# Two more key steps ahead of the value steps, key outputs in two pools, sample slots first in the gather

## The chip, the cores and the metric

One core of a Trainium2 chip runs the whole kernel. The metric is device time in microseconds (us) of one execution; lower is better. TensorE (PE) multiplies matrices, VectorE (DVE) and ScalarE (ACT) do elementwise work, GpSimd (POOL) does elementwise work and issues gathers, SyncE (SP) issues most loads.

## What is computed

One layer of a hybrid decoder, on 512 prompt tokens and 8 x 4 = 32 sample tokens, all in float32. The first part (recurrence, state space, gates) is not touched here. The second part is an expert mixer with 8 heads and 128 x 128 = 16384 single-neuron experts:

```python
# per head: the 16 best of 128 x 128 key pairs by summed score -> expert, gate = softmax
act = gelu(einsum('thkd,td->thk', u_tab[expert], x))
out = einsum('thk,thkd->td', gate * act, v_tab[expert])
y = rmsnorm(x_residual + out, final_norm_w)
```

## The kernel before

The mixer handles the tokens in two ways. Prompt tokens 128 to 511 (three tiles of 128, `d_tiles`) are done densely: for each of NE = 128 keys e, that is 128 experts each, a **key step** (`h_step(e)`) multiplies table u of that key with the 384 tokens and puts the gelu into a tile `gh[e]` of 128 x 384; a **value step** (`v_step(e)`) multiplies `gh[e]` with the routing weights (`wt`, read in blocks of eight keys from a scratch `Wt` in DRAM) and adds the product with table v of that key to three accumulators in PSUM. Tables are split in two float32r halves (`thi` by a ScalarE cast, `tlo` by a VectorE subtraction), so a key step is 8 x 3 matmuls of 384 columns and a value step 3 x 3 x 2 of 512. The first prompt tile (128 tokens, 128 slots each) and the samples (32 tokens laid out four times over the partitions, 32 slots) are `g_tiles` and are done by gather: `gathered` walks over 160 slots, and for each GpSimd fetches 128 rows of u and v (1 MB, three slots ahead); one step is VectorE's product with the token (L1353, `uv`) and ScalarE's gelu and gate (`w`), the next is VectorE's `acc` (L1360). At the end of a tile the four copies of the samples are folded by matmuls with `sid`, copied, and `finish` adds the residual row, normalizes and stores.

Nothing is scheduled by a planner: each engine runs its instructions in the order in which the program emits them. Background work is Python generators in the queues `bg` and `fill`; `tick(rate)` adds the rate to a debt, and for each whole unit one generator makes one step. A key step has four ticks (after k = 1, 3, 5, 7), a value step three. So the rates set how many gathered steps lie between the matmuls of a key.

The order of the mixer: `experts` runs AH = 34 key steps **ahead**, between the router's work (lists, top-k, `combine`), the building of `Wt` (`build_w`) and the samples' lists. Up to e = AH - AW = 22 they stand in the router's loop at rate 1, then ten in the building of `Wt`, then the last two. Their outputs need AH tiles `gh`: AH - 3 in a pool `gha`, the last three in `ghp`. Then the value steps run alone (`G_AHEAD` = 0.38 per tick) until 31 are done; the pool is closed, its room goes to the tables of the later key steps (`dpu2`), keys 34 and 35 are fetched, and the last weights and five residual rows (`finish_load`) are loaded in one go. From there a **loop** does key step v + 1 and value step v in turn with rate `G_RATE`, which is worked out so that the gather ends with the loop. `v_last` does the last value step, finishes the dense tiles and drains what is left of the gather.

Of the kernel before, what the change touches and what calls it, by code (L numbers as in the profile page):

```python
# [8 lines left out]
F32 = mybir.dt.float32  # L9
# [10 lines left out]
P = 128  # L20
D = 1024
# [69 lines left out]
def body(tc, a):  # L91
# [7 lines left out]
    def pool(st, name, bufs=1, right=False, space=None):  # L99
        kw = {} if space is None else {"space": space}  # L100
        return st.enter_context(tc.tile_pool(name=name, bufs=bufs, side="right" if right else "left", reuse_waits="tile", **kw))

    def load(dst, src):
        nc.sync.dma_start(dst, src)
# [23 lines left out]
    T_ = {}  # L128
# [1175 lines left out]
                            sm.rearrange("p (a b) -> p a b", a=na).unsqueeze(3).to_broadcast([P, na, nb, 16]), ALU.mult)  # L1304


    def finish_load(fp, t, rows, x2):
        o = fp.tile([P, D], F32, name="fin", tag=f"fin{t}")
        load(o[:rows], x2)
        return o  # L1310

# [17 lines left out]
    def gathered(gp, ps_of, tiles):  # L1329

        slots = [(i, k) for i, t in enumerate(tiles) for k in range(t[1][2])]
        uvs, accs = {}, {}

        def fetch(j):
            if j < len(slots):
                i, k = slots[j]
                ei = tiles[i][1][0]
                uvs[j] = gp.tile([P, 2 * D], F32, name="uv", tag="uv", bufs=GA)
                PO.indirect_dma_start(out=uvs[j], out_offset=None, in_=a["uv"],  # L1339
                                      in_offset=bass.IndirectOffsetOnAxis(ap=ei[:, k : k + 1], axis=0))  # L1340

        for x in range(GA - 1):
            fetch(x)
        yield
        for j, (i, k) in enumerate(slots):
            rows, (ei, gate, n), h2, end = tiles[i]
            if k == 0:
                accs[i] = gp.tile([P, D], F32, name="acc", tag="acc", bufs=1)
            acc = accs[i]
            w = gp.tile([P, 1], F32, name="w", tag="w", bufs=4)  # L1350
            fetch(j + GA - 1)
            uv = uvs.pop(j)
            V.scalar_tensor_tensor(out=uv[:, 0:D], in0=uv[:, 0:D], scalar=1.0, in1=h2, op0=ALU.mult, op1=ALU.mult, accum_out=w)  # L1353
            AC.activation(w, w, AF.Gelu)  # L1354
            AC.mul(w, w, gate[:, k : k + 1])  # L1355
            yield
            if k == 0:
                AC.mul(acc, uv[:, D:], w)
            else:
                V.scalar_tensor_tensor(acc, uv[:, D:], w, acc, ALU.mult, ALU.add)  # L1360
            yield
            if k == n - 1:
                o2 = acc.rearrange("p (a b) -> p a b", a=2)
                if rows < P:
                    for b in range(2):
                        ps = ps_of()
                        mm(ps[:rows, :512], T_["sid"], acc[:, 512 * b : 512 * b + 512], start=True, stop=True)
                        yield
                        AC.copy(acc[:rows, 512 * b : 512 * b + 512], ps[:rows, :512])
                    yield  # L1370
                    o2 = acc[:rows].rearrange("p (a b) -> p a b", a=2)
                yield from end(o2)


    NE = 128
    AH = 34
    GA = 4
    VB = 3
    W0E = PO
# [11 lines left out]

    G_AHEAD = 0.38
    G_END = -8
    G_RATE = (2 * 160 + 12 - 3 * (AH - 1) * G_AHEAD) / (7 * (NE - AH) - 3 * G_END)

    def build_w(bp, pw, io, sls, Wt, w0):

# [40 lines left out]
    def experts(h2s, x2s, h2pair, ph, g_tiles, d_tiles, outs, s, ghp, es, sq):  # L1438
        nd = len(d_tiles)
        nt = nd * P  # L1440
        c0 = ph.p0 + d_tiles[0] - ph.t0
        Wt = dram.tile([nt // TB, P, P * TB], F32, name="Wt")
        st_ = ExitStack()
        ga = pool(st_, "gha")
        dps = ExitStack()
        dp = pool(dps, "dpu")
        php = pool(es, "php", 2, space=PSUM)
# [2 lines left out]
        def ps_h():  # L1450
            return php.tile([P, 512], F32, name="hps", tag="h")
# [3 lines left out]
        def fetch(kind, e):  # L1455
            if e < NE and (kind, e) not in raws:
                t = (dp if kind == "u" else dv).tile([P, D], F32, name="traw", tag="traw" + kind, bufs=2 if kind == "u" else VB)
                load(t, a["uT"][e] if kind == "u" else a["uv"][e * P : (e + 1) * P, D : 2 * D])
                raws[kind, e] = t
# [14 lines left out]
        def prep_lo(kind, e):  # L1474
            if e < NE and (kind, e) in raws:
                x, y = sp_[kind, e]
                (PO if kind == "u" and e < sum(AQ) else V).tensor_tensor(y, raws.pop((kind, e)), x, ALU.subtract)  # L1477
                if kind == "v" or e + 2 not in (AH, AH + 1) or e >= AH:
                    fetch(kind, e + (2 if kind == "u" else VB))

        gh = {}

        def h_step(e, rate, lo_at=0):
            prep("u", e)
            if e + 1 != AH:
                fetch("u", e + 1)
                prep("u", e + 1, True)
            x, y = sp_.pop(("u", e))
            ps = ps_h()
            for k in range(KT):  # L1490
                ks = slice(k * P, k * P + P)
                cs = slice(c0, c0 + nt)
                mm(ps[:, :nt], x[:, ks], hi[:, k, cs], start=(k == 0), stop=False)  # L1493
                mm(ps[:, :nt], x[:, ks], lo[:, k, cs], start=False, stop=False)  # L1494
                mm(ps[:, :nt], y[:, ks], hi[:, k, cs], start=False, stop=(k == KT - 1))  # L1495
                if k % 2:
                    (bg if e < AH else fill).tick(rate)
                if k == lo_at and e + 1 != AH:
                    prep_lo("u", e + 1)
            gh[e] = ga.tile([P, nt], F32, name="gh", tag="gh", bufs=AH - 3) if e < AH - 3 else ghp.tile([P, nt], F32, name="gh", tag="gh", bufs=3)  # L1500
            AC.activation(gh[e], ps[:, :nt], AF.Gelu)

        gs = {}
# [64 lines left out]
        e = 0  # L1568
# [60 lines left out]
        rows_of = {t: NS if t is None else P for t in g_tiles + d_tiles}  # L1629
        fins = {}  # L1630
        fill.add(gathered(gp, ps_h, [(rows_of[t], res[t], h2s[t], end_of(t, rows_of[t])) for t in g_tiles]))

        def v_of(v, rate):
            if v % 8 == 0:
                fetch_w(v // 8 + 1)
            v_step(v, rate)

        for v in range(AH - 3):
            v_of(v, G_AHEAD)
        st_.close()  # L1640
        dp = pool(es, "dpu2")
        fetch("u", AH)
        fetch("u", AH + 1)
        v_of(AH - 3, G_AHEAD)
        prep("u", AH)
        v_of(AH - 2, G_AHEAD)
        fp = T_["fp"] = pool(es, "fp")
        T_["fwbc"] = fp.tile([P, D], F32, name="fwbc")
        load(T_["fwbc"], a["fw"].to_broadcast([P, D]))
        for t in g_tiles + d_tiles:  # L1650
            fins[t] = finish_load(fp, t, rows_of[t], x2s[t])
        h_step(AH, G_RATE)
        for v in range(AH - 1, NE - NL):
            if AH < v + 1 < NE:
                h_step(v + 1, G_RATE)
            v_of(v, G_RATE)
        for v in range(NE - NL + 1, NE):
            h_step(v, G_RATE)
        v_last(range(NE - NL, NE))
        es.close()  # L1660

    outs = {None: a["o_y_s"]}
    for t in range(0, SEQ, P):
        outs[t] = a["o_y_p"][t : t + P]
    ph = Phase(0, True, 0, SEQ, True)
    g_tiles, d_tiles = [0, None], [128, 256, 384]
    es, sq = ExitStack(), ExitStack()
    wq = Stream(None, None, [(WQ0 + i, None, 0, None, PO) for i in range(16)], 4, Q_RATE, 0)
    h2s, x2s, h2pair, ghp = network(ph, g_tiles, wq, es, sq)
# [94 lines left out]
```

## Time and profile before

| | us |
|---|---|
| time, median of 3 runs | 2227.87 (2227.82 to 2234.36) |
| time of the profiled execution | 2235.91 |
| its span, first to last instruction | 2234.2 |
| PE busy, of the span | 2112.2 (95%) |
| DVE busy | 1578.4 (71%) |
| ACT busy | 848.8 (38%) |
| mean granted clock of TensorE, as a share | 0.981 |

The profile gives each engine's instructions with start and length. Matmuls overlap and their ends are modelled, so a TensorE that is busy all the time is not necessarily at its peak; distances between starts are the safer measure. The ahead stage lies at about 885 to 1237 us, the value steps alone at 1237 to 1382, the loop at 1382 to 2208.

### The profile page before, as it was taken

The numbers are of one execution on the slowest core, as the hardware profiler recorded it, in microseconds if no ns is written. First come the engines' busy times: TensorE is split into PE (matmuls) and PEld (weight loads), VectorE is DVE, ScalarE is ACT, GpSimd is POOL, SyncE is SP. The second block draws the span as 40 slices with busy tenths as digits, with TensorE's granted clock in tenths as the row PEclk, the third lists the DMA queues.
The fourth block names the chain that finished last, engine by engine and source line by source line (L and its number), as shares of the span: only waits on it lengthen the run. The fifth ranks groups of instructions, "written<-read, shape, count | busy, mean of one in ns | idle before, by whom it ended". The sixth has DMA issues, their size and how long they took to land.

```text
span 2234.2 us, 34565 instructions
## 1 busy us (share of the span) xinstructions
PE 2112.2 (95%) x13085; PEld 1937.5 (87%) x13085; DVE 1578.4 (71%) x3056; ACT 848.8 (38%) x1583; POOL 815.8 (37%) x904
## 2 busy tenths in 40 slices
PE   7899998999999998999899999899999999999996
PEld 6889898898999998999799878788888888888885
DVE  6866566655445424799998778687778788777777
ACT  3323232333113324333477434343443433344343
POOL 3488762224443333664166111222222222222221
PEclk9999998999999999999999999999999999999998
DMA  4433344326644243232356979899889999888983
GB/s 147 121 111 119 123 126 137 113 100 186 200 134 129 88 151 121 81 109 68 111 227 260 332 276 331 308 335 334 326 309 333 334 331 333 309 330 312 331 300 148
DMA packets 199814, 478.90 MB, mean 214 GB/s; under 512 B 53440, under 2 KB 114752, under 8 KB 176096
## 3 DMA queue, kind: packets, MB, share of 16 engines
q1 hardware_dynamic: 169136, 278.50, 37.6%
q0 software_dynamic: 24752, 170.67, 20.3%
q10 hardware_dynamic: 5760, 27.53, 3.1%
q8 instruction: 103, 1.69, 0.3%
q14 instruction: 63, 0.52, 0.1%
HBM read 419.42 MB, written 54.46 MB: 212 GB/s over the span
## 4 chain that ended last, share of the span: by engine, by line
PE 53%; DVE 26%; issue 8%; ACT 7%; DMA 5%; POOL 1%; SPq 0%; DVEq 0%; POOLq 0%; ACTq 0%
PE gps L469 23%; PE eacc L1548 7%; DVE uv L1353 5%; DVE tlo L1477 5%; PE hps L1493 3%; PE hps L1495 3%; PE hps L1494 3%; DVE acc L1360 3%; ACT thi L1469 3%; PE pw L1428 3%; DMA traw<-in_uv 2%; DVE glo L483 2%; PE aps L605 1%; ACT w L1355 1%; PE py L790 1%
## 5 line engine op out<-in xcount | busy, mean ns | idle before, releaser
L469 PE MATMUL gps<-pr,wh 128*128 128x272 f32 (+1 forms) x3328 | 584.7, 298 | 5.8 <-DVE pr L483 3.2
L469 PEld LDWEIGHTS gps<-pr,wh 128*128 128x128 f32 x3328 | 481.7, 192 | 14.5 <-issue 4.4
L1477 DVE TENSOR_TENSOR tlo<-traw,thi 128x1024 fp32r<-128x1024 f32 x241 | 298.9, 1241 | 146.3 <-ACT thi L1469 146.3
L1339 POOL DMA_INDIRECT uv<-in_uv,ei x128 | 176.4, 1378 | 605.4 <-DVE acc L1360 578.1
L469 PE MATMUL gps<-pr,wl 128*128 128x272 f32 (+1 forms) x1664 | 354.4, 293 | 8.8 <-POOL wl L435 7.7
L1495 PE MATMUL hps<-pr,tlo 128*128 128x384 f32 x1024 | 348.5, 340 | 15.0 <-DVE tlo L1477 13.5
L1493 PE MATMUL hps<-pr,thi 128*128 128x384 f32 x1024 | 350.8, 343 | 8.6 <-ACT thi L1469 8.6
L435 POOL TENSOR_TENSOR wl<-wraw,wh 128x1024 fp32r<-128x1024 f32 x88 | 216.9, 2465 | 350.8 <-ACT wh L434 338.9
L1494 PE MATMUL hps<-pr,thi 128*128 128x384 f32 x1024 | 344.5, 336 | 0.0
L1469 ACT CAST thi<-traw 128x1024 fp32r<-128x1024 f32 x256 | 266.1, 1040 | 44.5 <-DMA traw<-in_uv 15.6
L469 PEld LDWEIGHTS gps<-pr,wl 128*128 128x128 f32 x1664 | 267.3, 192 | 9.9 <-POOL wl L435 8.2
L1548 PE MATMUL eacc<-thi,ghi 128*128 128x512 f32 x768 | 243.7, 398 | 10.6 <-ACT ghi L482 9.4
L1548 PE MATMUL eacc<-tlo,ghi 128*128 128x512 f32 x768 | 243.4, 398 | 4.1
L1548 PE MATMUL eacc<-thi,glo 128*128 128x512 f32 x768 | 238.5, 392 | 0.0
L1360 DVE SCALAR_TENSOR_TENSOR acc<-uv,w,acc 128x1024 f32<-128x1024 f32 x158 | 202.3, 1280 | 30.5 <-ACT w L1355 30.5
L1354 ACT ACTIVATE w<-w 128x1 f32<-128x1 f32 x160 | 32.5, 203 | 486.3 <-DVE uv L1353 486.3
L1495 PEld LDWEIGHTS hps<-pr,tlo 128*128 128x128 f32 x1024 | 192.9, 188 | 23.0 <-DVE tlo L1477 21.8
L1493 PEld LDWEIGHTS hps<-pr,thi 128*128 128x128 f32 x1024 | 193.4, 189 | 15.8 <-ACT thi L1469 10.7
L1494 PEld LDWEIGHTS hps<-pr,thi 128*128 128x128 f32 x1024 | 193.4, 189 | 3.6
L1353 DVE SCALAR_TENSOR_TENSOR uv<-uv,h 128x1024 f32<-128x1024 f32 x160 | 194.8, 1217 | 0.0
L1548 PEld LDWEIGHTS eacc<-tlo,ghi 128*128 128x128 f32 x768 | 141.9, 189 | 50.1 <-DVE tlo L1477 21.9
L1548 PEld LDWEIGHTS eacc<-thi,ghi 128*128 128x128 f32 x768 | 141.2, 189 | 46.6 <-ACT ghi L482 22.6
(405 smaller groups left out, 3021.5 us busy)
## 6 DMA issues: line engine op xcount, KB each, us to landing
traw<-in_uT SPq DMA_DIRECT2D x128, 512.0 KB
traw<-in_uv SPq DMA_DIRECT2D x128, 512.0 KB
wraw<-in_W SPq DMA_DIRECT2D x104, 512.0 KB
Wt<-wb ACTq DMA_DIRECT2D x24, 1024.0 KB
wt<-Wt SPq DMA_DIRECT2D x15, 1536.0 KB
st<-in_state_hgrn SPq DMA_DIRECT2D x8, 512.0 KB
Wd<-W SPq DMA_DIRECT2D x8, 512.0 KB
ATd<-AT SPq DMA_DIRECT2D x8, 512.0 KB
```

The costliest lines, as they stand in the source:

```text
L435: E.tensor_tensor(wl, r3, wh, ALU.subtract)
L469: mm(ps[:, b, :w], x[:, k], y[:, k, b * w : b * w + w], start=(k == 0 and x is wh and y is hi), stop=(k == KT - 1 and x is wl))
L1339: PO.indirect_dma_start(out=uvs[j], out_offset=None, in_=a["uv"], in_offset=bass.IndirectOffsetOnAxis(ap=ei[:, k : k + 1], axis=0))
L1353: V.scalar_tensor_tensor(out=uv[:, 0:D], in0=uv[:, 0:D], scalar=1.0, in1=h2, op0=ALU.mult, op1=ALU.mult, accum_out=w)
L1360: V.scalar_tensor_tensor(acc, uv[:, D:], w, acc, ALU.mult, ALU.add)
L1428: mm(pt[:, t], o2[:, t], o1[:, t], start=True, stop=True)
L1469: AC.copy(x, t)
L1477: (PO if kind == "u" and e < sum(AQ) else V).tensor_tensor(y, raws.pop((kind, e)), x, ALU.subtract)
L1493: mm(ps[:, :nt], x[:, ks], hi[:, k, cs], start=(k == 0), stop=False)
L1494: mm(ps[:, :nt], x[:, ks], lo[:, k, cs], start=False, stop=False)
L1495: mm(ps[:, :nt], y[:, ks], hi[:, k, cs], start=False, stop=(k == KT - 1))
L1548: mm(accs[d][:, b], l[:, ds_], r[:, b * 512 : b * 512 + 512], start=st, stop=en)
```

## The change

AH goes from 34 to 36, so keys 34 and 35 move out of the loop to the steps ahead, and value steps 33 and 34 into the stage of value steps alone. The outputs `gh` of keys 0 to 17 (AT = 18) stand in the pool `gha`, those of 18 to 32 in a fixed tile `gb`, the last three in `ghp` as before. The pool is closed after value step 17, and the tables of keys 36 and 37 are fetched there. `gb` stays to the end: its six parts take the final weights and the five residual rows, which are now loaded one at a time in the loop (the weights at v = 37, then a row at v = 40, 44, 48, 52, 56). The samples' slots are walked through before those of the first prompt tile, and three empty steps stand between the samples' last slot and their folding. `G_RATE` follows from AH and the constant 15 for 12: 0.4316 before, 0.4418 after.

```diff
-    def finish_load(fp, t, rows, x2):
-        o = fp.tile([P, D], F32, name="fin", tag=f"fin{t}")
+    def finish_load(o, rows, x2):
         load(o[:rows], x2)
         return o
@@ gathered
                 if rows < P:
+                    yield
+                    yield
+                    yield
                     for b in range(2):
@@
-    AH = 34
+    AH, AT = 36, 18
-    G_RATE = (2 * 160 + 12 - 3 * (AH - 1) * G_AHEAD) / (7 * (NE - AH) - 3 * G_END)
+    G_RATE = (2 * 160 + 15 - 3 * (AH - 1) * G_AHEAD) / (7 * (NE - AH) - 3 * G_END)
@@ experts
-        ga = pool(st_, "gha")
+        gb = pool(st_, "ghb").tile([P, 6, D], F32, name="gb")
+        gbf = gb.rearrange("p a b -> p (a b)")
+        gts = ExitStack()
+        ga = pool(gts, "gha")
@@ h_step
-            gh[e] = ga.tile([P, nt], F32, name="gh", tag="gh", bufs=AH - 3) if e < AH - 3 else ghp.tile([P, nt], F32, name="gh", tag="gh", bufs=3)
+            if e < AT:
+                gh[e] = ga.tile([P, nt], F32, name="gh", tag="gh", bufs=AT)
+            elif e < AH - 3:
+                gh[e] = gbf[:, (e - AT) * nt : (e - AT + 1) * nt]
+            else:
+                gh[e] = ghp.tile([P, nt], F32, name="gh", tag="gh", bufs=3)
@@ experts
-        for v in range(AH - 3):
+        for v in range(AT):
             v_of(v, G_AHEAD)
-        st_.close()
+        gts.close()
         dp = pool(es, "dpu2")
         fetch("u", AH)
         fetch("u", AH + 1)
-        v_of(AH - 3, G_AHEAD)
+        for v in range(AT, AH - 2):
+            v_of(v, G_AHEAD)
         prep("u", AH)
         v_of(AH - 2, G_AHEAD)
         fp = T_["fp"] = pool(es, "fp")
-        T_["fwbc"] = fp.tile([P, D], F32, name="fwbc")
-        load(T_["fwbc"], a["fw"].to_broadcast([P, D]))
-        for t in g_tiles + d_tiles:
-            fins[t] = finish_load(fp, t, rows_of[t], x2s[t])
+        T_["fwbc"] = gb[:, 0]
         h_step(AH, G_RATE)
+        late = deque(enumerate(g_tiles + d_tiles))
         for v in range(AH - 1, NE - NL):
+            if v == AH + 1:
+                load(T_["fwbc"], a["fw"].to_broadcast([P, D]))
+            if v >= AH + 2 and v % 4 == 0 and late:
+                i, t = late.popleft()
+                fins[t] = finish_load(gb[:, i + 1], rows_of[t], x2s[t])
@@
-    g_tiles, d_tiles = [0, None], [128, 256, 384]
+    g_tiles, d_tiles = [None, 0], [128, 256, 384]
```

## Rows read from the trace of the kernel before

**Rows 1.** Busy time by stage; the first row names the columns; last, 10 us.

```profile
core 0: us, PE busy (x) PEld busy (x) DVE busy (x) ACT busy (x) POOL busy (x), PEclk, DMA share, GB/s
...
1045.00:1092.00 47.00, 37.34 (x204) 34.99 (x203) 44.28 (x172) 16.57 (x26) 0.00 (x0) 0.93 0.27 93
...
1237.00:1382.00 145.00, 138.86 (x593) 111.27 (x594) 109.53 (x150) 58.88 (x105) 21.67 (x21) 0.98 0.87 309
1382.00:1421.00 39.00, 31.53 (x151) 28.42 (x151) 23.38 (x30) 10.92 (x22) 7.42 (x5) 0.91 0.93 337
1421.00:2208.00 787.00, 772.54 (x3800) 675.22 (x3799) 625.10 (x771) 315.00 (x635) 194.61 (x135) 1.00 0.88 319
...
1240.00:1250.00 10.00, 10.00 (x46) 8.28 (x45) 6.12 (x10) 4.37 (x7) 2.70 (x3) 1.00 1.02 412
```

**Rows 2.** The chain that ended last: start us, length us, what.

```profile
1237.56 28.91 PE eacc L1548 x126
...
1393.26 20.10 DMA traw<-in_uT
...
1772.70 0.17 PE hps L1493
...
1776.88 4.11 PE eacc L1548 x18
...
1786.43 1.20 DVE acc L1360
...
1820.98 1.20 DVE acc L1360
```

**Rows 3.** Timeline of DVE in the loop: start, length, operation, [idle before, releaser].

```profile
1771.40 1.22 DVE L1353 SCALAR_TENSOR_TENSOR uv<-uv,h 128x1024 f32<-128x1024 f32 x1
...
1773.22 1.28 DVE L1360 SCALAR_TENSOR_TENSOR acc<-uv,w,acc 128x1024 f32<-128x1024 f32 x1 [0.60 <-ACT w L1355]
...
1779.25 1.22 DVE L1477 TENSOR_TENSOR tlo<-traw,thi 128x1024 fp32r<-128x1024 f32 x1 [1.53 <-ACT thi L1469]
...
1783.79 0.56 DVE L1510 TENSOR_TENSOR gh<-gh,wt 128x384 f32<-128x384 f32 x1 [0.97 <-ACT gh L1501]
1784.73 1.23 DVE L1477 TENSOR_TENSOR tlo<-traw,thi 128x1024 fp32r<-128x1024 f32 x1 [0.38 <-ACT thi L1469]
```

**Rows 4.** Timeline of PE: three stops, and starts of value steps.

```profile
1088.05 1.34 PE L1591 MATMUL pt<-c_ident,r_all 128*128 128x128 f32 x4 [6.04 <-DVE r_all L1301]
...
1292.22 1.22 PE L1548 MATMUL eacc<-thi,ghi 128*128 128x512 f32 x2 [5.37 <-ACT ghi L482]
...
1414.48 0.69 PE L1493 MATMUL hps<-pr,thi 128*128 128x384 f32 x1 [7.22 <-ACT thi L1469]
...
1421.25 0.63 PE L1548 MATMUL eacc<-thi,ghi 128*128 128x512 f32 x2
...
1541.83 0.63 PE L1548 MATMUL eacc<-thi,ghi 128*128 128x512 f32 x2
...
1550.32 0.73 PE L1548 MATMUL eacc<-thi,ghi 128*128 128x512 f32 x2
...
1560.66 0.63 PE L1548 MATMUL eacc<-thi,ghi 128*128 128x512 f32 x2
...
2020.15 0.63 PE L1548 MATMUL eacc<-thi,ghi 128*128 128x512 f32 x2
...
2074.39 0.73 PE L1548 MATMUL eacc<-thi,ghi 128*128 128x512 f32 x2 [0.54 <-ACT ghi L482]
...
2204.19 0.63 PE L1548 MATMUL eacc<-thi,ghi 128*128 128x512 f32 x2
```

**Rows 5.** Timeline of SP, which issues the loads: start, length, what.

```profile
1390.08 2.32 SPq L104 DMA_DIRECT2D fin<-x  x5
1393.26 0.33 SPq L104 DMA_DIRECT2D traw<-in_uT  x1
```

**Rows 6.** Timeline of DVE at the end.

```profile
2225.76 1.27 DVE L1325 SCALAR_TENSOR_TENSOR fin<-fin,ss,fwbc 32x1024 f32<-32x1024 f32 x1 [0.65 <-POOL ss L496]
```

More of the change, by code (lines that the diff above doesn't have):

```diff
@@ L1660, in experts @@
         es.close()
+        st_.close()
     outs = {None: a["o_y_s"]}
```

## The prediction, made before the changed kernel was run

> **What bounds the kernel now.** Read the table by stage first [rows 1]. Up to 1045 us the change touches nothing. From 1045 to 1092 (the router's last lists) VectorE is busy 44.28 of 47 us and TensorE 37.34. From 1237 to 1382 only value steps run: 594 weight loads are 33 steps of 18, so 145/33 = 4.39 us a step. From 1382 to 1421 (151 loads: about four key steps of 24 and three value steps) TensorE is busy 31.53 of 39. From 1421 to 2208 a key step and a value step alternate, and TensorE looks full at 772.54 of 787.
>
> Then the chain of waits. A key step spans 1772.70 to 1776.88 = 4.18 us and a value step 4.11 us [rows 2], so a key needs 8.29 us of TensorE; seven value steps in a row take 28.91, 4.13 each. But the same VectorE operation returns at 1786.43 and 1820.98 [rows 2]: 34.55 us for four keys, 8.64 a key. TensorE is not the bound there. VectorE's own timeline over two keys [rows 3] shows four waits, all for ScalarE: 0.60 + 1.53 + 0.97 + 0.38 = 3.48 of 17.28 us. ScalarE runs in order and sits behind w, which needs the product of a gathered row (uv, 1.22 us) from VectorE. So the loop goes at the pace of a VectorE-ScalarE ring, and each gathered step that a key carries lengthens it.
>
> Last, where TensorE really stops: 6.04 us at 1088 for the router's r_all, 5.37 us at 1292, 7.22 us at 1414 [rows 4]. The last one is the late tables: five residual rows go out at 1390.08, ahead of the table issued at 1393.26, which takes 20.10 us [rows 2, 5].
>
> **The change part by part**, against the profiled execution (span 2234.2 us, own time 2235.9; the median of the three runs is 2227.87, 0.3% lower, so I carry the difference over, not the level).
>
> *Two more key steps early.* The router's loop ends at key AH-12, so it takes keys 22 and 23 as well; what follows keeps its number of steps. TensorE needs 2 x 4.18 = 8.4 us, of which it idles 6.04 us there now [rows 4]. VectorE is the bound in that stage, and each key step puts one tlo of 1.22 us on it [rows 3], in front of the reductions that r_all waits for; the second tlo must also wait for its cast. So 2.4 us plus about 1.3 of waiting, less about 1 because the transposes at 1088 (1.34 us for four after an idle) come sooner after matmuls (the granted clock of this stage is 0.93 [rows 1]): +2.8. Bounds: 2.4 - 1.3 = +1.1, and +8.4 if nothing hides. Their table loads run where the DMA share is 0.27 [rows 1]. [...]
>
> *Two more value steps in the stage without key steps*: between 4.13 [rows 2] and 4.39 [rows 1]; 2 x 4.2 = +8.4.
>
> *Tables of keys 36 and 37 fetched after value step 17* (about 1322 us) instead of after step 30. 1 MB more enters SP's queue ahead of the next value table; the value tables are three ahead and the stage's DMA share is 0.87 [rows 1]. The bounds are 0 and one short TensorE stop of the kind at 1292 cut to the 3 us that 1 MB takes at 337 GB/s; I take +0.5, since no row shows a stop after 1292 in this stage.
>
> *Transition without residual loads.* Now 39 us. Four key steps and three value steps at the loop's pace are 3 x 8.64 + 4.18 = 30.1; the first key of the new loop carries four gathered steps, part of which VectorE, idle before, absorbs: 30.8. So -8.0 (0 if the stop stays, -9.2 at best). The lateness has nowhere to go: the residual rows now go one per four keys.
>
> *The loop.* Before, value step 36 starts at 1421.25 and 126 at 2204.19 [rows 4]: 782.9 us for 90 keys. After, 88 keys x 8.64 = 760.3. But the same 160 gathered slots must pass in fewer keys: G_RATE rises from 0.4316 to 0.4418, and seven ticks a key are 3.02 before and 3.09 after. Counting the ticks through Tasks.tick, the old loop has two keys with four steps (50 and 97), the new one seven past the transition and the samples' end (57, 68, 79, 90, 101, 111, 122). What one costs is in the trace: value steps 50, 51, 52 start at 1541.83, 1550.32, 1560.66 [rows 4], so the two keys take 18.83 instead of 17.28: +1.55. Seven are 10.9 (bounds: 0 if the gaps of 3.48 us take them; 7 x (1.55 + 0.60) = 15 where uv and its acc stand side by side and VectorE waits 0.60 [rows 3]). The samples' end moves from the tail into keys 43 to 46: two folding matmul pairs, two ScalarE copies, a finish of VectorE and ScalarE work and a GpSimd power, ahead of the next gather in GpSimd's queue. Prompt tile 0's finish does the like now: steps 105 to 111 start at 2020.15 and 2074.39 [rows 4], 54.2 for six keys of 8.64 = 51.8, so +2.4. Three empty yields lighten VectorE; the matmuls weigh on TensorE. I take +3 (0 to 6). Loop: 760.3 + 10.9 + 3 = 774.2, so -8.7.
>
> *Residual rows and the final weights, spread over keys 37 to 56.* 0.5 MB per four keys is 15 GB/s on top of 319 [rows 1]; the prefetched tables hide it. It costs if the tables' slack is gone, which is the second rival. The trace reaches 412 GB/s over 10 us [rows 1]. The Trainium skill (HBM Reference, Specifications) gives about 358 GB/s as a core's effective share, while saying that a core streaming alone gets more. By 358 the three residual loads that share their key with a 1.5 MB weight load would delay the tables 1.5 us each, 4.4 us in all if it all showed; the row says that the cap does not bind here, and the sum has 0.
>
> *The tail.* Now 2204.19 to 2234.2 = 30.0. The last finish ends at 2225.76 + 1.27 [rows 6], VectorE being nearly gapless before it. The old tail holds one slot (uv and acc) and the samples' end, the new one two and a half slots and the finish of prompt tile 0. That is three more VectorE operations of 1.22 to 1.28 and one more wait of 0.60 [rows 3]: +4.4. The two folding matmuls and copies leave the tail, but VectorE's work covered them. The last store grows from 128 to 512 KB, at 337 GB/s about 1 us, part of it overlapped: +0.6. Together +5.0 (2 to 6).
>
> **Sum:** 2.8 + 8.4 + 0.5 - 8.0 - 8.7 + 5.0 = 0.0. Two keys leave the loop (-17.3) and the stop goes (-8.0). Against that stand the same keys' steps done early (+11.2), the early loads (+0.5), the tail (+5.0), and the loop's time above 8.64 a key, which grows from 782.9 - 777.6 = 5.3 to 13.9 (+8.6).
>
> **Rivals.**
> 1. *The denser steps are free.* ScalarE's waits leave VectorE 3.48 us in two keys [rows 3]; if a fourth step fills a gap, the 10.9 us go: 2228 - 11 = 2217. For it: the gaps are there. Against it: the key measured with four steps paid 1.55 us, and the ring and not VectorE's busy time sets the pace. Chance 0.33.
> 2. *Late tables in the loop: slower.* Residual loads at keys 40, 48 and 56 are issued just before the 1.5 MB weight load of the same key, all in SP's queue, with the next tables behind them. The value step at 1292 shows what a table behind a weight load costs when it comes too late: 5.37 us of idle [rows 4], and about 1 us of slower matmuls after it. It decides once a table lands after the cast that needs it. Two such stops are 2 x 6.4 = 12.8: 2241. For it: DMA share 0.88 in the loop [rows 1]. Against it: in the loop VectorE's rows [rows 3] show waits for ScalarE's order alone and none behind a table, although weight loads come every eight keys. Chance 0.15.
> 3. *The change does not do what it says: the stop stays.* The weight load of key 32 and the next tables alone fill the queue for 10 us, and 8 us of stop remain at the new transition: 2236. The residual rows, 2.1 MB of what was queued, speak against it. Chance 0.07.
> 4. *The forecast*, all terms near the values taken: 0.45.
>
> **How the numbers follow.** About 0.3% (6.7 us) is what a measurement here can tell from no change, and the forecast, 2228, lies within it. Rival 1 is faster by more (0.33), rivals 2 and 3 slower (0.22), the rest the same (0.45). The range must leave out no more than 0.2, so it reaches to rival 1's 2217 and near rival 2's 2241: 2216 to 2240.
>
> **What would show it.** Right: the start of the value steps some 3 us later; TensorE without the 7.22 us stop; fewer keys at 8.64 us with a jump of about 1.5 us each eleven keys; a tail of about 35 us. Wrong: an idle of TensorE at 1330 or in keys 37 to 57 behind a table (rival 2 or 3); a loop at 8.64 us without the jumps (rival 1). What would spoil the sum most is the ring: if the moved steps give it another order, its 8.64 us changes, and 0.1 us a key is 9 us.

## The result and the profile after

The changed kernel takes 2215.94 us (median of four runs, 2212.16 to 2217.47) beside 2230.74 us of the kernel before measured with it (2227.82 to 2234.36): a ratio of 0.9933, 95% interval 0.9916 to 0.9951. It is faster by about 15 us. The forecast was 2228, no change; the time lies just under the lower end of the range given, 2216.

The profiled execution took 2217.47 us. Its head (busy us, share of the span, instructions):

```profile
span 2215.7 us, 34563 instructions
PE 2104.8 (95%) x13085; PEld 1938.3 (87%) x13085; DVE 1579.0 (71%) x3056; ACT 848.8 (38%) x1583; POOL 818.5 (37%) x904
```

Against the profiled execution of before the span is 18.5 us shorter: TensorE is busy 7.4 us less, with the same matmuls, and idle 11.1 us less. VectorE is busy as long as before. The busy times by stage say where; the windows end at the starts of value steps, and the columns are those of [rows 1]:

```profile
1045.00:1096.00 51.00, 45.92 (x262) 43.73 (x261) 47.41 (x175) 20.41 (x32) 0.53 (x1) 1.00 0.30 108
1240.75:1382.45 141.70, 140.80 (x613) 113.93 (x613) 114.81 (x157) 59.31 (x105) 22.20 (x22) 1.00 0.93 329
1382.45:1415.54 33.09, 33.09 (x169) 30.20 (x168) 25.92 (x34) 13.95 (x28) 8.19 (x5) 1.00 0.97 351
1415.54:2181.61 766.07, 751.22 (x3702) 657.95 (x3701) 607.90 (x749) 308.03 (x619) 193.65 (x133) 1.00 0.88 323
2181.61:2215.70 34.09, 8.78 (x37) 6.34 (x36) 23.65 (x33) 9.20 (x23) 4.80 (x5) 0.69 0.30 118
```

They are, in order: the router's end, value steps 0 to 33 alone, the transition (value steps 34 to 37 and their key steps), the loop from value step 38 to 126, and the tail. In the transition TensorE is busy in all of its 33.09 us, at a granted clock of 1.00; before, the like stretch had 0.91 [rows 1] and a stop of 7.22 us [rows 4].

Two executions of one program differ by some us at places that no edit touches: the value steps start at 1246.1 us in one trace and at 1234.1 in another whose code is the same up to there (e7 and e8 below), and the 5.37 us stop at 1292 [rows 4] is not in a second trace of the kernel before (e1 below), whose value steps are 7 us quicker for it. So stages are compared from the start of value step 0, and e1 stands for before. A is the number of key steps ahead; the transition is value steps A - 2 to A + 2:

| trace | gelu of key 15 to value 0 | value 0 to A - 2 | transition | loop to value 126 | tail |
|---|---|---|---|---|---|
| before | 185.5 | 140.6 | 43.1 | 782.9 | 30.0 |
| e1, before again | 184.8 | 133.7 | 44.0 | 782.7 | 30.0 |
| after | 188.4 | 141.7 | 33.1 | 766.1 | 34.1 |
| e13, after again | 188.2 | 142.7 | 33.1 | 765.9 | 34.1 |

After against e1: +3.6 in front, +8.0 in the value steps, -10.9 in the transition, -16.6 in the loop, +4.1 in the tail: -11.8 us. The front scatters most: over all traces of this document it takes 184.3 to 190.2 us with A = 34 and 187.2 to 191.1 with A = 36, with medians of 184.8 and 188.3.

The loads around the transition, from SP's timeline of after (start, length, what; one of the tables, `traw`, is 0.5 MB, a block of weights, `wt`, 1.5 MB):

```profile
1374.15 0.43 SPq L104 DMA_DIRECT2D wt<-Wt  x1
1378.15 3.94 SPq L104 DMA_DIRECT2D traw<-in_uv  x2
1385.80 0.33 SPq L104 DMA_DIRECT2D traw<-in_uT  x1
...
1405.06 0.44 SPq L104 DMA_DIRECT2D gb<-in_fw  x1
```

The weights of value step 32 are followed by ordinary tables alone, and the final weights come 31 us later. In the kernel before, the same block was followed within 8 us by the final weights and five residual rows. That is SP's timeline in e1, and below it the chain of waits of e1 and TensorE's stop:

```profile
1374.24 0.64 SPq L104 DMA_DIRECT2D wt<-Wt  x1
...
1380.89 0.42 SPq L104 DMA_DIRECT2D fwbc<-in_fw  x1
1381.36 2.31 SPq L104 DMA_DIRECT2D fin<-x  x5
1384.56 0.33 SPq L104 DMA_DIRECT2D traw<-in_uT  x1
```

```profile
1366.30 5.20 DMA traw<-in_uT
...
1374.24 10.26 DMA wt<-Wt
...
1384.56 21.11 DMA traw<-in_uT
```

```profile
1406.79 0.69 PE L1493 MATMUL hps<-pr,thi 128*128 128x384 f32 x1 [7.99 <-ACT thi L1469]
```

The tables issued at 1366.30 had landed after 5.20 us; the one issued at 1384.56 takes 21.11, and TensorE stands still for 7.99 us. The prediction saw the residual rows in this; the block of weights ahead of them is what its sum passed over (rival 3 alone names it), and the experiments had to say which of the two makes the stop.

### The profile page after: what moved, and what is told of

Read it like the earlier page. It is cut to its first block, busy times and chain, and to the rows that moved or that the text cites. A ratio compares the mean times of both kernels' runs of the same rounds, so it can differ in the third digit from the quotient of the medians.

```text
span 2215.7 us, 34563 instructions
## 1 busy us (share of the span) xinstructions
PE 2104.8 (95%) x13085; PEld 1938.3 (87%) x13085; DVE 1579.0 (71%) x3056; ACT 848.8 (38%) x1583; POOL 818.5 (37%) x904
## 5 line engine op out<-in xcount | busy, mean ns | idle before, releaser
L469 PEld LDWEIGHTS gps<-pr,wh 128*128 128x128 f32 x3328 | 484.2, 193 | 14.2 <-issue 4.2
L1338 POOL DMA_INDIRECT uv<-in_uv,ei x128 | 186.1, 1454 | 534.9 <-DVE acc L1359 527.3
L1558 PEld LDWEIGHTS eacc<-tlo,ghi 128*128 128x128 f32 x768 | 141.5, 188 | 46.3 <-DVE tlo L1482 17.8
```

The source lines that it names most:

```text
L469: mm(ps[:, b, :w], x[:, k], y[:, k, b * w : b * w + w], start=(k == 0 and x is wh and y is hi), stop=(k == KT - 1 and x is wl))
L1558: mm(accs[d][:, b], l[:, ds_], r[:, b * 512 : b * 512 + 512], start=st, stop=en)
```

## The experiments

Two readings of the gain were open after the first comparison. In the prediction's, the residual rows alone stood ahead of the table, so taking them apart removes the stop whatever else is done. In the other, the pile counts: a block of weights and the lump of rows and a table that is needed soon, all within a few us in SP's queue; breaking any one link is then enough. Beside it stood the question what the other parts of the change (order of the slots, two more steps ahead) are worth. Medians are given beside those of the kernel before in the same batch: 2229.18 for e1 to e4, 2229.45 for e5 to e8, 2229.16 for e9 to e12, 2228.45 for e13 to e15; ratios carry their 95% intervals.

**e1, the kernel before again.** No edit.

> The kernel before, unchanged, profiled once more. Its first trace has a stop of TensorE of 5.37 us at 1292 us (value step 12), the trace after the change has none; from value step 11 to 13 the two differ by 7.6 us. Theory A (the stop comes and goes between executions): the step is as likely without the stop, span then about 2226 to 2228 us; the runs of before at 2227.8 and at 2234 are these two kinds. Theory B (the stop belongs to this order of slots and loads): it stands again at step 12, some 5 us, span about 2234 us.

Measured 2228.64 us, ratio 1.0002 (0.999 to 1.0014). The stop in the transition is there (7.99 us, above), the one at 1292 is not. So the first is of the kernel, the second of that one execution.

**e2, the order of the slots alone**, put into the kernel before:

```diff
                 if rows < P:
+                    yield
+                    yield
+                    yield
...
-    G_RATE = (2 * 160 + 12 - 3 * (AH - 1) * G_AHEAD) / (7 * (NE - AH) - 3 * G_END)
+    G_RATE = (2 * 160 + 15 - 3 * (AH - 1) * G_AHEAD) / (7 * (NE - AH) - 3 * G_END)
...
-    g_tiles, d_tiles = [0, None], [128, 256, 384]
+    g_tiles, d_tiles = [None, 0], [128, 256, 384]
```

> The kernel before with only the order of the gather changed: samples' slots first, three empty steps, constant 15. AH stays 34, the residual rows are loaded in one go. Theory B (the order takes the stop at step 12 away, and the samples' end in mid-loop gives VectorE room): about 7 us at step 12 and about 2 us in keys 43 to 56 less, tail some 4 us longer, so 2223 to 2229 us against 2231 of before. Rival (the gain is all AH and the loads): within 3 us of before or slower by the tail's 4 us, 2231 to 2235 us; the stop at 1414 us stays in both.

Measured 2231.56 us, ratio 1.0008 (0.9997 to 1.002). Transition 43.1, loop 782.0, tail 34.3: the tail's +4.3 stands alone, with 0.7 us from the loop against it. Nothing is gained by the order.

**e3, the change without the order of the slots:** the same lines taken back in the changed kernel.

```diff
-                    yield
-                    yield
-                    yield
...
-    G_RATE = (2 * 160 + 15 - 3 * (AH - 1) * G_AHEAD) / (7 * (NE - AH) - 3 * G_END)
+    G_RATE = (2 * 160 + 12 - 3 * (AH - 1) * G_AHEAD) / (7 * (NE - AH) - 3 * G_END)
...
-    g_tiles, d_tiles = [None, 0], [128, 256, 384]
+    g_tiles, d_tiles = [0, None], [128, 256, 384]
```

> The kernel after with only the order undone: prompt tile 0 first, no empty steps, constant 12; AH 36, two homes, early tables, residual rows apart stay. If the order is worth what the traces show (5 us of the loop at the samples' end and, if theory B holds, 7.6 us at step 12, less 4 us of tail): 2222 to 2226 us. Rival (order worth nothing, loads and AH are all): 2214 to 2218 us.

Measured 2215.47 us, ratio 0.9931 (0.9915 to 0.9948): the time of the change. Transition 33.1; loop 768.6 and tail 29.9 in place of 766.1 and 34.1: 2.5 us more in the one, 4.2 less in the other. The gain owes nothing to the order.

**e4, the change with 34 key steps ahead:**

```diff
-    AH, AT = 36, 18
+    AH, AT = 34, 18
```

> The kernel after with AH back at 34 (order, two homes, early tables at value step 18, residual rows apart stay). My sum for the two keys: +2.8 ahead, +8.4 value steps, -17.3 loop, +9 denser steps, so +3 us for 36 against 34: without them 2211 to 2216 us, no slower than after. Rival (the two keys are the gain, the loop's 8.64 us a key being what is saved): 2224 to 2230 us.

Measured 2217.20 us, ratio 0.9947 (0.9931 to 0.9964). Transition 33.1, loop 780.1 for 90 keys, front 184.3. The stop is gone without the two extra steps, and 1.3 us separate this kernel from the whole change, less than its runs scatter.

**e5, residual rows in one go, in the changed kernel:**

```diff
         T_["fwbc"] = gb[:, 0]
+        load(T_["fwbc"], a["fw"].to_broadcast([P, D]))
+        for i, t in enumerate(g_tiles + d_tiles):
+            fins[t] = finish_load(gb[:, i + 1], rows_of[t], x2s[t])
         h_step(AH, G_RATE)
-        late = deque(enumerate(g_tiles + d_tiles))
         for v in range(AH - 1, NE - NL):
-            if v == AH + 1:
-                load(T_["fwbc"], a["fw"].to_broadcast([P, D]))
-            if v >= AH + 2 and v % 4 == 0 and late:
-                i, t = late.popleft()
-                fins[t] = finish_load(gb[:, i + 1], rows_of[t], x2s[t])
```

> The kernel after, but the final weights and the five residual rows are loaded in one go ahead of key step 36, as before the change; the early fetch of tables 36 and 37 stays. Theory (the residual rows' 2.6 MB in front of the next tables made the stop): the stop comes back near key step 38 or 39, value step 34 to 38 takes 43 us in place of 33, time 2222 to 2227 us. Rival (the early fetch took the stop away): 33 to 35 us, 2214 to 2218 us.

Measured 2217.67 us, ratio 0.9949 (0.9926 to 0.9972); transition 34.2. The rows are back in one lump, yet no stop comes back. By itself that speaks against the prediction's reading. SP's timeline shows what is different from e1:

```profile
1367.95 0.43 SPq L104 DMA_DIRECT2D wt<-Wt  x1
...
1382.17 3.46 SPq L104 DMA_DIRECT2D gb<-x  x5
1386.65 0.33 SPq L104 DMA_DIRECT2D traw<-in_uT  x1
```

The lump goes out at the end of value step A - 2, the weights at step 32. With A = 36 these are two steps apart: 14.2 us from the weights to the rows, against 7.1 us in e1. The table behind the rows is still slow, but hardly too late: issued at 1386.65, it releases ScalarE's cast at 1404.21, 17.6 us later, and the cast waited 2.40 us for it where e1's waited 13.83:

```profile
1404.21 1.05 ACT L1474 CAST thi<-traw 128x1024 fp32r<-128x1024 f32 x1 [2.40 <-DMA traw<-in_uT]
```

**e6, the tables of keys 36 and 37 fetched late,** in the changed kernel:

```diff
         dp = pool(es, "dpu2")
+        for v in range(AT, AH - 3):
+            v_of(v, G_AHEAD)
         fetch("u", AH)
         fetch("u", AH + 1)
-        for v in range(AT, AH - 2):
-            v_of(v, G_AHEAD)
+        v_of(AH - 3, G_AHEAD)
```

> The kernel after, but tables 36 and 37 are fetched after value step 32, as late as before the change; the residual rows stay apart. Theory (the residual rows made the stop): value steps 34 to 38 take 33 to 35 us, 2214 to 2219 us. Rival (the late fetch made it): 41 us or more, 2222 to 2227 us.

Measured 2223.02 us, ratio 0.9966 (0.9952 to 0.9981); transition 42.9. A stop is back with no residual row anywhere near: first SP's timeline, then ScalarE's, then TensorE's.

```profile
1373.36 0.43 SPq L104 DMA_DIRECT2D wt<-Wt  x1
1377.36 5.09 SPq L104 DMA_DIRECT2D traw<-in_uv  x1
1382.51 0.90 SPq L104 DMA_DIRECT2D traw<-in_uT  x2
```

```profile
1391.03 1.99 ACT L1474 CAST thi<-traw 128x1024 fp32r<-128x1024 f32 x2 [8.25 <-DMA traw<-in_uT]
```

```profile
1392.13 0.69 PE L1498 MATMUL hps<-pr,thi 128*128 128x384 f32 x1 [6.24 <-ACT thi L1474]
```

At A = 36 the late place lies behind the weights of step 32; in the kernel before it lay ahead of them (e1 issued these tables at 1366.30). SP itself is held there: the first table that it issues behind the weights takes it 5.09 us, where a table otherwise takes 0.3 to 0.5, so the two tables that are needed leave only at 1382.51, and ScalarE gets them 8.5 us later. So the early fetch is what the extra steps need, and the pile can be made of other loads than the rows. No run moves the weights by themselves; that they make this stop rests on e10 below, where the same late place, ahead of the weights, has none.

**e7 and e8, more gathered steps ahead:** e3's lines, and the rate of the stage in which value steps run alone, 0.45 in e7 and 0.55 in e8.

```diff
-    G_AHEAD = 0.38
+    G_AHEAD = 0.45
```

> The kernel of e3 (order undone) with G_AHEAD 0.45 for 0.38: the loop then holds 260 gathered steps of uv or acc in keys 38 to 125 in place of 267, the stage of value steps alone seven more. From the pairs before/e3 and e4/after, 2c + 3t = 14 us and c + 3t = 8.64 give t = 1.1 us a step: loop 768.6 - 7.6 = 761 us, the stage ahead unchanged, time 2206 to 2210 us. With my forecast's 1.55 a step only for the five keys with four steps: 760.8 us, the same. Rival (VectorE's ring does not care for the number of steps): 768 us. Rival (the stage ahead pays, its DMA share being 0.87): its 35 steps take 150 us or more in place of 142.

> As e7 with G_AHEAD 0.55: 251 gathered steps in the loop, 16 fewer than e3. At 1.1 us each 751 us (TensorE's floor of 8.28 a key is 729); with the forecast's price, where only keys with more than three steps cost extra, it would stay at 761. The stage ahead moves 8 MB more: at 340 GB/s that is 24 us of transfers more in a stage whose share is 0.87, so it must grow from 142 to some 150 us. Time 2203 to 2212 us.

Measured 2207.53 us for 0.45, ratio 0.9911 (0.9881 to 0.994), and 2210.57 for 0.55, ratio 0.9929 (0.9902 to 0.9956). The windows of the value steps and of the loop, first of e7, then of e8:

```profile
1246.07:1394.35 148.28, 144.58 (x612) 111.97 (x613) 121.24 (x166) 61.00 (x114) 29.89 (x25) 1.00 0.93 335
1427.77:2184.05 756.28, 747.55 (x3697) 658.26 (x3697) 602.73 (x745) 306.74 (x615) 190.05 (x131) 1.00 0.89 325
```

```profile
1234.05:1397.22 163.17, 150.22 (x612) 109.06 (x612) 133.13 (x181) 62.63 (x123) 36.51 (x30) 1.00 0.94 337
1432.40:2175.47 743.07, 739.54 (x3698) 660.14 (x3697) 590.13 (x728) 303.90 (x605) 178.19 (x125) 1.00 0.89 324
```

Against e3 (141.5 and 768.6), 0.45 pays 6.8 us ahead and saves 12.3 in the loop; 0.55 pays 21.7 and saves 25.5. In e8 TensorE is idle for 13 us of the value steps (163.17 - 150.22), in pieces of about 1 us or less behind ScalarE, such as this one:

```profile
1314.95 0.73 PE L1555 MATMUL eacc<-thi,ghi 128*128 128x512 f32 x2 [0.78 <-ACT ghi L482]
```

The other 9 us are in matmuls that show longer (TensorE is busy 150.22 us, against 140.80 for the same 34 steps in after); no run says why. From 0.45 to 0.55 the price ahead grows by 14.9 us and the saving by 13.2, so nothing more is to be had there.

**e9, rows in one go with 34 steps ahead** (e4's and e5's edits together): the run that separates the readings. With A = 34 the lump falls right behind the weights again, but the tables for the transition were fetched early.

```diff
-    AH, AT = 36, 18
+    AH, AT = 34, 18
...
+        load(T_["fwbc"], a["fw"].to_broadcast([P, D]))
+        for i, t in enumerate(g_tiles + d_tiles):
+            fins[t] = finish_load(gb[:, i + 1], rows_of[t], x2s[t])
...
```

> e4 (AH 34, early tables, order new) with the final weights and the five residual rows again in one go ahead of key step 34. Before the change they stand 8 us behind the 1.5 MB weight load of value step 32, in e5 (AH 36) 14 us behind it. Theory P (the pile of weight load, rows and next table made the stop; any one of them moved breaks it): the pile is whole again, the stop returns, value steps 32 to 36 take 40 to 44 us, loop and tail as e4, time 2224 to 2228 us. Theory E (early tables alone break it): 33 to 35 us, 2216 to 2220 us.

Measured 2230.11 us, ratio 1.0003 (0.9987 to 1.0018): the whole gain is lost. Transition 43.0. SP's timeline and TensorE's stop:

```profile
1372.40 0.43 SPq L104 DMA_DIRECT2D wt<-Wt  x1
...
1377.52 0.43 SPq L104 DMA_DIRECT2D gb<-in_fw  x1
1377.99 2.32 SPq L104 DMA_DIRECT2D gb<-x  x5
1381.15 0.33 SPq L104 DMA_DIRECT2D traw<-in_uT  x1
```

```profile
1403.66 0.69 PE L1498 MATMUL hps<-pr,thi 128*128 128x384 f32 x1 [6.43 <-ACT thi L1474]
```

The same lump costs 10 us here and 1 us in e5; the rows are 5.6 us behind the weights here, 14.2 there. Counted from the start of value step A - 2 (1368.15 here, 1376.29 in e5), the table behind the rows is issued after 13.0 us here and after 10.4 in e5, and is used 21.4 us later here and 17.6 in e5. So nearness to the weights costs twice, in when SP gets to the table and in how long the table takes.

**e10, the kernel before with its residual rows loaded apart,** and no other part of the change:

```diff
-    def finish_load(fp, t, rows, x2):
-        o = fp.tile([P, D], F32, name="fin", tag=f"fin{t}")
+    def finish_load(o, rows, x2):
...
-        load(T_["fwbc"], a["fw"].to_broadcast([P, D]))
-        for t in g_tiles + d_tiles:
-            fins[t] = finish_load(fp, t, rows_of[t], x2s[t])
+        ft = {t: fp.tile([P, D], F32, name="fin", tag=f"fin{t}") for t in g_tiles + d_tiles}
         h_step(AH, G_RATE)
+        late = deque(g_tiles + d_tiles)
         for v in range(AH - 1, NE - NL):
+            if v == AH + 1:
+                load(T_["fwbc"], a["fw"].to_broadcast([P, D]))
+            if v >= AH + 2 and v % 4 == 0 and late:
+                t = late.popleft()
+                fins[t] = finish_load(ft[t], rows_of[t], x2s[t])
```

> The kernel before with only the residual rows and the final weights loaded apart, as after the change; AH 34, late tables, old order. Theory P: the pile is broken by this alone, value steps 32 to 36 take 33 to 35 us in place of 44, time 9 to 11 us under before, 2218 to 2221 us. Theory E (the late tables are the cause): 42 to 44 us, no faster than before.

Measured 2216.30 us, ratio 0.9941 (0.9921 to 0.9961). Its transition, with the weights still where they were:

```profile
1368.20:1401.30 33.10, 33.10 (x170) 30.21 (x168) 26.13 (x33) 14.52 (x28) 8.18 (x5) 1.00 1.03 385
```

These few lines alone give 12.9 us, nearly the whole gain of the change (14.8 us in the first comparison, 13.8 in e13). The queue is still there: the DMA share is 1.03, and the table behind the weights, issued at 1378.66, takes 12.07 us in the chain of waits, against 5.20 for the one at 1366.30 in e1 and 21.11 behind the rows. But without the rows the tables land in time.

```profile
1378.66 12.07 DMA traw<-in_uT
```

**e11, the change without the three empty steps:**

```diff
                 if rows < P:
-                    yield
-                    yield
-                    yield
```

> The kernel after without the three empty steps, same G_RATE. The loop then holds 267 gathered steps from key 38 to 125 in place of 264, the tail 2 in place of 5. If a gathered step costs the same wherever it lies: loop 766.1 + 3 x 1.1 to 1.6 = 769 to 771 us, tail 34.1 - 4 = 30 us, time within 2 us of after. Rival (the empty steps themselves make the fast keys 45 to 55, as my reading of the stretch at 8.28 us a key has it): three steps of 1.55 us are thirteen keys times 0.36, so the stretch shrinks from eleven keys to at most three.

Measured 2223.37 us, ratio 0.9983 (0.9963 to 1.0003); the loop takes 777.2 in place of 766.1. TensorE's timeline at the folding:

```profile
1463.01 1.89 PE L1366 MATMUL hps<-acc,c_sid 128*32 128x512 f32 x2 [5.00 <-DVE acc L1359]
```

The folding matmul stands in TensorE's queue right behind the last gathered step and holds up the key's matmuls until VectorE's `acc` is done: 5.00 us. The key takes 15.75 us from value step 42 to 43, 7.1 above 8.64. The other 4 of the 11 us fit three gathered steps which, by the program's order, fall into the loop here and not into the tail; that takes 30.4. Behind the stop nine keys (44 to 52) run at TensorE's own pace, 8.28 us each, as after's keys 45 to 54 do:

```profile
1475.16:1549.68 74.52, 74.52 (x379) 67.97 (x379) 57.82 (x73) 30.75 (x60) 20.19 (x14) 1.00 0.88 317
```

The rival gave the stretch at most three keys, so the empty steps are not needed for it; here the stop itself may have let VectorE and ScalarE get ahead.

**e12, a rate of 0.42 ahead** (e7's edit with that number).

> As e7 with G_AHEAD 0.42: 263 gathered steps in the loop's keys 38 to 125, one key with four. From e3 (267 steps, 768.6 us) and e7 (260, 756.3): 1.76 us a step, so 761 to 764 us; the stage ahead between 141.5 (e3) and 148.3 (e7), say 144; time 2207 to 2213 us. Rival (the stage ahead pays back what the loop saves): no less than e3's 2215 us.

Measured 2215.31 us, ratio 0.9933 (0.9908 to 0.9957): value steps 146.8, loop 761.3, between e3 and e7 in the loop but not in the time, which is that of e3. In these single traces the price ahead comes sooner than the saving.

**e13, the changed kernel again,** without an edit.

> The kernel after, unchanged, beside e14 and e15 on one chip: 2214 to 2217 us; loop 766, value steps 34 to 38 33.1 us. It gives the direct comparison that the earlier runs lack.

Measured 2214.65 us, ratio 0.994 (0.9921 to 0.996). Every stage repeats within 1 us (the table above).

**e14, e7 again**, beside e13 on the same chip.

> e7 once more (AH 36, order undone, G_AHEAD 0.45). From first value step to the end its trace is 967.9 us against after's 975.0: 2207 to 2210 us, 6 to 8 us under after, if each gathered step that leaves the loop saves about 1.55 us there and the stage ahead pays back half of it. Rival (e12's 2215 is the rule and e7's median was luck): within 2 us of after.

Measured 2207.26 us, ratio 0.9915 (0.9894 to 0.9936): 7.4 us below e13. So the change with the old order of slots and a rate of 0.45 is faster than the kernel before in both runs, and than the changed kernel where the two stood side by side.

**e15, e10 with the rate of 0.45:** the kernel before with e10's lines, 34 steps ahead, and

```diff
-    G_AHEAD = 0.38
+    G_AHEAD = 0.45
```

> e10 (the kernel before, residual rows loaded apart, AH 34) with G_AHEAD 0.45: 263 gathered steps in 90 keys, 2.92 a key. By 1.55 us a step e10's loop of 781 us becomes 781 - 7 x 1.55 = 770 us, the stage ahead grows by 5 to 7 us, so 5 us under e10: 2209 to 2213 us. If the two keys moved ahead are worth nothing (as e4 and e10 say), it equals e14 within 3 us; if they are worth 3 us or more, it lies that much above e14.

Measured 2214.55 us, ratio 0.9942 (0.9921 to 0.9963): against e10's 2216.30 the rate brings no clear gain here. From value step 0 to the end it takes 975.0 us, e14 967.1, while e14 pays 3.9 more in front of it: by stages the two extra steps ahead are worth 4.0 us at this rate, of the 7.3 us between the medians; at 0.38 (e4 beside the change, e10 beside e3) they were worth 1 to 2 us, within the scatter.

## Why the prediction was wrong

**Right.** The bound of the loop, the ring of VectorE and ScalarE, fits what was measured: taking gathered steps out of the loop shortens it where TensorE's work stays the same (e3, e7, e8: 768.6, 756.3, 743.1 us for the same 88 keys). The front steps were put at +2.8 and measured +3.6 and +3.4; the router's stop fell from 6.04 us [rows 4] to 1.09:

```profile
1091.70 1.09 PE L1601 MATMUL pt<-c_ident,r_all 128*128 128x128 f32 x5 [1.09 <-DVE r_all L1301]
```

VectorE, the full engine there, is busy 47.41 us in the window to 1096 us, 3.1 more than in [rows 1], about what the front grew by. The Trainium skill (Perfetto Trace Analysis, Optimization Strategy) says that interleaving stretches with different limits may improve performance. The trace agrees: work that takes TensorE 8.4 us was done for 3.6, though not for nothing. The value steps were put at +8.4 and measured +8.0, the early fetch at +0.5 and nothing of it was seen, the tail at +5.0 and measured +4.1. VectorE's last finish is where the tail's 4.1 us came from; it was expected to carry 4.4 of the 5.0:

```profile
2207.42 1.28 DVE L1324 SCALAR_TENSOR_TENSOR gb<-gb,ss 128x1024 f32<-128x1024 f32 x1 [0.66 <-POOL ss L496]
```

From value step 126 to its end are 27.1 us, against 22.8 in [rows 4, 6]; behind it both kernels take 7 us, so the larger last store, put at 0.6, cost nothing. Rival 2, late tables in the loop behind the spread rows, did not come: keys 40, 48 and 56, where a row goes out ahead of a block of weights, take 8.80, 8.28 and 8.51 us in after, and e10, which spreads the same rows, gains as much. The three loads that 358 GB/s (the Trainium skill, HBM Reference, Specifications) would have delayed show no delay, and e10's transition moves 385 GB/s for 33 us.

**The step that failed most: the loop, forecast at 774.2 us, measured 766.1 (-8.1).** 88 keys at 8.64 us are 760.3 of that; the time above it was to grow from 5.3 to 13.9 us and measured 5.8. Of its terms, seven denser keys were put at 10.9 us and the samples' end at 3.

- The samples' end (keys 43 to 54) was put at 12 x 8.64 + 3 = 106.7 us and took 101.7, for after two keys of 9.46 and 9.45 us came ten at TensorE's own pace. This is their window:

```profile
1477.17:1559.97 82.80, 82.80 (x421) 75.41 (x421) 63.39 (x80) 34.50 (x69) 22.53 (x15) 1.00 0.87 315
```

  82.80 us for ten keys, with TensorE busy all the time: 8.28 a key. Keys 43 and 44 carry one gathered product and one `acc` between them, so VectorE and ScalarE get ahead; the ten that follow carry 27 gathered steps (14 products, 13 `acc`, one of them ScalarE's), not 30, and it seems that they live on that lead, at 0.36 us a key. e10 does the same after its transition: keys 36 to 42 at 8.28 each. The three empty steps are not needed for it: e11 has the stretch without them, though behind a stop of TensorE. That it is a lead which is used up is the reading that fits; no run measured it by itself.
- The denser keys do come, one region each eleven keys, as forecast, but at less: keys 55 to 125, with all seven, take 8.2 us more than 8.64 each, where 10.9 was forecast. Key 112 shows it plainest. Value step 112 starts at 2057.36, and TensorE's timeline has the next two:

```profile
2067.70 0.63 PE L1558 MATMUL eacc<-thi,ghi 128*128 128x512 f32 x2
...
2075.98 0.63 PE L1558 MATMUL eacc<-thi,ghi 128*128 128x512 f32 x2
```

```profile
2057.36:2075.98 18.62, 17.51 (x84) 14.92 (x85) 15.13 (x20) 6.93 (x14) 4.36 (x3) 1.00 0.94 324
```

  10.34 us for the key with four steps and 8.28 for the next. Below TensorE's two starts stands the window of both: 18.62 us, 1.34 above 2 x 8.64, where 1.55 was taken from [rows 4], and TensorE idle for 1.11 of them.
- Behind the larger part lies one error of counting: seven keys were made denser without taking off the gathered steps that the samples' end and the tail take out of the loop, and the tail's were priced a second time there, at +5.0. Counted through the program's order, as the prediction counted its denser keys, the loop carries 264 gathered steps in 88 keys, and it carried 270 in 90: three a key both times. The windows of `acc`, every second step, say the same: VectorE has 131 of 132 in after and below it 134 of 135 in before, and the first `acc` of a tile, one in each window, is ScalarE's:

```profile
1415.54:2181.61 766.07, 167.52 (x131) 1.00 0.88 323
```

```profile
1421.25:2204.19 782.94, 171.56 (x134) 1.00 0.88 321
```

  So the loop could not grow denser on the whole. A sum from the prediction's own rows, 8.64 us a key plus 1.55 for each step above three a key (less 1.55 for each below), comes near all four loops: 777.6 of 782.7 measured for e1, 760.3 of 766.1 for after; with 260 steps in e7 and 251 in e8, 754.1 of 756.3 and 740.2 of 743.1. The remainder is 2 to 6 us in all four, and no run takes it apart.

**The second: the transition, forecast at -8.0, measured -10.9 against e1** (-10.0 against the trace that the forecast was made from, and past its bound of -9.2). The prediction's own terms, 39 and 30.8, give -8.2. The stop went whole, and the keys behind it ran at TensorE's 8.28, four of them in 33.1 us, where 8.64 and a price for the fourth gathered step were counted. And its cause was named by half. It was put on the five residual rows ahead of the table. The rows alone do little harm (e5, 34.2) when they come two value steps behind the weights; late tables behind the weights do, without rows (e6, 42.9); weights and rows together make the stop (e1, e9), and the rows apart remove it (e10). So rival 3 (the stop stays because of the weights of key 32) named the other half of the pile. The stop was rightly forecast to go, since the change breaks the pile twice, by rows apart and by the shift of A.

**The sum.** The loop, 7.9 us under its forecast, and the transition, 2.9 under, make 10.8 of the 11.8 us by which after's trace is shorter than e1's, where the sum said 0; the other terms are within 1 us each. Put differently, the prediction let the rest of the change eat up the 8 us of the stop. Measured, the rest costs about nothing: from value step 0 to the end after takes 975.0 us and e10, which has the rows apart and nothing else, 978.3, and in front after pays about 3.5 more. Rival 1 gave 2217 us, close to the time measured, but by a mechanism that the runs don't show: the fourth gathered step is not free.

**What each part is worth** (e2, e3, e4, e10, e13): residual rows apart, -13 us, nearly the whole gain; two more steps ahead with the early fetch, -1 to -2 us, not clear of the scatter; the order of the slots, 0, at a tail that is 4 us longer. The two homes for the outputs are what makes the early fetch and A = 36 fit; they weren't tried apart from these.

**A faster version.** A = 36, rows apart, the old order of slots and a rate of 0.45: 2207.5 and 2207.3 us, ratios 0.9911 and 0.9915.

## What to carry to other kernels

Before you name the load that makes a table late, list all that stands ahead of it in its queue and the distance to it: a lump is harmful or not by what it follows, and an edit that moves it two steps away can do as much as taking it apart. When work is moved between stages, count it once over the whole span (what one stage loses, another must show) before any price is put on its density. And where two engines that wait for each other pace a loop, count the filler steps in it: here fewer of them made the loop shorter each time (e3, e7, e8), while the stage that took them in paid back more than half of it at 0.45 and most of it at 0.55, and with 34 steps ahead (e15) the gain was not clear of the scatter.

## What the runs showed of the hardware

- A 0.5 MB table took 5.2 us to land at 1366.30 and 21.1 us at 1384.56 in the same trace of e1; between them 1.5 MB of weights, 2.6 MB of final weights and residual rows and four other tables had gone out from the same engine.
- The first load that SP issued behind that 1.5 MB took it 5.37 us to issue in e1, 4.92 in e10, 5.09 in e6 and 3.85 in e9, where a table otherwise takes 0.3 to 0.5.
- Executions of one and the same program differ in places: the kernel before had a stop of 5.37 us at value step 12 in one trace and none in another, and the value steps start 12 us apart in e7 and e8, with the same code up to there. So a difference of 5 us in one stage of a single trace was no evidence here without a second one.
- In the transition the granted clock was 0.88 over e1's 44 us, with a stop in it, and 1.00 over e10's 33.1 us without one. This is e1's window; the granted clock is the number behind POOL's:

```profile
1369.71:1413.75 44.04, 35.79 (x169) 32.05 (x168) 25.73 (x32) 13.31 (x25) 7.45 (x5) 0.88 0.93 332
```

  From 1405 to 1410 us, at the end of the 7.99 us in which TensorE did nothing and just behind them, it was 0.50, the lower of its two levels (1.2 and 2.4 GHz):

```profile
1405.00:1410.00 5.00, 2.96 (x8) 2.46 (x9) 2.63 (x4) 1.84 (x5) 0.00 (x0) 0.50 0.56 191
```

  Part of what a stop costs is this: matmuls of 384 columns show 0.69 us right behind it, against 0.34 us in the same stage of the changed kernel:

```profile
1386.53 0.34 PE L1498 MATMUL hps<-pr,thi 128*128 128x384 f32 x1
```
